# Two layers of a hybrid decoder on one core: index products in pairs of banks, and a head with its loads, gates and decay rows at other places

## The chip, the cores and the metric

The kernel runs on one core of one Trainium2 chip. A core has five engines, each with its own queue of instructions: TensorE (PE, matrix products and transposes), VectorE (DVE, element-wise work and reductions), ScalarE (ACT, functions and copies), GpSimd (POOL) and SyncE (SP), which issues the DMA transfers. An engine runs its queue in order; where an instruction needs another engine's result, it waits on a semaphore, and everything behind it in its queue waits too. TensorE's results land in PSUM banks, from which ACT and DVE read them. The metric is the device time of one launch in microseconds (us), lower is better.

## The reference, cut to what matters

Two layers, each a token mixer and a SwiGLU feed-forward part, over 256 tokens of width 1024. Each is normed and scaled by a conditioning vector, which is the product of `silu(c)` with `w_mod`:

```python
mod = c_act @ w_mod[l] + b_mod[l]               # 1024 x 6144 per layer
sh_m, sc_m, g_m, sh_f, sc_f, g_f = jnp.split(mod, 6, axis=-1)
h = rms_norm(x, mix_norm_pre[l]) * (1.0 + sc_m[:, None, :]) + sh_m[:, None, :]
y = hybrid_mixer(h, ...)
```

The mixer joins eight attention heads with four mLSTM heads. The attention looks only at 64 keys per query, which an indexer picks; the index has eight heads of depth 64:

```python
idx_logits = jnp.einsum('thd,sd->ths', qib, ki32)
idx_score = jnp.einsum('ths,th->ts', jax.nn.relu(idx_logits), wib)
idx_score = jnp.where(key_pos[None, :] <= t[:, None], idx_score, -jnp.inf)
_, sel = lax.top_k(idx_score, n_sel)            # n_sel = 64, blocks of 128 queries
```

The mLSTM heads need, per token, an input gate and the running sum of a log forget gate, from which a running maximum (the "stabiliser") and a matrix of decays follow.

## The kernel before, in words

**Head of a layer (L449 to L603).** `mixer` first issues what the gates, index and queries need. `between(n)` (called at several places) fetches the next pieces of `w_mod` (1 MB each, tile `wm`, two rows of 1024 per partition) and multiplies them into an accumulator `macc` with one DVE operation per row: L189 for the first row of a block, L191 (a multiply and add) for the others. `HEAD[l]` says how many pieces each such call takes. In order there come: the product `pki` (index keys and gate columns, weights `wsm`), its copy `kix`, the rotary product `kir`, the transposes `pwif`, then the gate block (transposes `pgt`, gates `ga`/`gc`, two scans, the maximum `M`, its rounded copy `Mp` and the remainder), the keys' product `pka` in two halves (`k_att(0,0)`, `k_att(0,1)`, weights `wka`), and the query products `pqidx` and `pq` (weights `wup`) with their rotary parts. A rotary part is a copy on ACT (`...x`), a product with `perm` on PE (`...p`), a product with `cosT` on POOL or DVE, one with `sinT` on DVE (`...b`, L358) and an addition (L359). The second transfer of keys' weights, the pieces of the next conditioning block, and the weights `wqk` come behind these.

**Order.** The rest of the layer is written as a list of steps (`ORDER[l]`): `w` is `decays()`, `e` is `k_att(1, m)`, `v` is a product of values, `i` the top-k of one block of queries, `r` the keys' rotary part, `l`, `t`, `u` the attention's logits, weights and products. A mark `~` says whether a step may start before the last matmul of the step ahead of it in the order of issue. The order on each engine is settled when the program is built: a scheduler with a model of durations places every instruction.

**Index products (L637 to L660).** For 128 queries of block `i` and 128·(i+1) keys, `index_part(i, b)` fills one PSUM bank `pi` of 512 columns: four heads of block 0, or two of block 1; a head's 64 rows lie in the lower or the upper half of the partitions (`p0 = 64 * (hd % 2)`). ACT takes the bank through a Relu (`rl`, L651), and DVE adds each head, times its weight, to the score `sc` (L656, L658). `inside` (L843) calls six of these, each after two of the 16 steps of a product of keys (layer 0) or values (layer 1). The order of heads is `HEADS[i]`. The top-k is a chain of pairs MAX8 and MATCH_REPLACE8 on DVE (L668, L669), eight per block of queries; the attention's logits `pl` are masked into `lm` (L709), their maximum `mx` taken (L712), and the exponentials go to the transposes `pT`.

**Decay rows (L609 to L634).** `decays()` transposes the gates (`pu`), copies them (`uc`), and multiplies the rows `Mp` with a selection (`pM`); ACT makes the decays `W` from `pM`.

Of the kernel before, what the change touches and what calls it, by code (L numbers as in the profile page):

```python
# [11 lines left out]
F32 = mybir.dt.float32  # L12
# [7 lines left out]
P = 128  # L20
# [36 lines left out]
def tile_hybrid_decoder(ctx: ExitStack, tc: tile.TileContext, a, out):  # L57
# [384 lines left out]
    HEAD = ((2, 2, 1, 1), (3, 2, 1, 0, 0))  # L442
# [3 lines left out]
    def mixer(l, h, between, early, hook, hf=None):  # L446
# [112 lines left out]
        k_att(0, 0)  # L559
        k_att(0, 1)  # L560
# [48 lines left out]
        def decays():  # L609
            pu = bankA(nm + "pu")  # L610
# [26 lines left out]
        def index_part(i, b):  # L637
            w_ = P * (i + 1)
            per = 512 // w_
            h0 = b * per  # L640
            if b == 0:
                score[i] = work.tile([P, S], F32, tag="score", name=f"{nm}sc{i}")
            sc = score[i]
            ps = bankA(f"{nm}pi{i}{h0}")
            for g in range(per):
                hd = HEADS[i][h0 + g]
                p0 = 64 * (hd % 2)
                mm = matmul(ps[:, g * w_:(g + 1) * w_], qT["qidx"][p0:p0 + 64, hd // 2, i * P:(i + 1) * P],
                                      kidx[p0:p0 + 64, 0, :w_], start=True, stop=True)
            rl = t2k(f"{nm}rl{i}{h0}")  # L650
            nc.scalar.activation(rl, ps, AF.Relu)  # L651
            for g in range(per):
                hd = HEADS[i][h0 + g]
                s = rl[:, g * w_:(g + 1) * w_]
                if h0 + g == 0:
                    nc.vector.tensor_scalar_mul(sc[:, :w_], s, wi[:, i, hd:hd + 1])  # L656
                else:
                    nc.vector.scalar_tensor_tensor(sc[:, :w_], s, wi[:, i, hd:hd + 1], sc[:, :w_], op0=ALU.mult, op1=ALU.add)  # L658
            return mm
# [183 lines left out]
        inside = {2 * b + 2: (lambda b=b: index_part(*((0, b) if b < 2 else (1, b - 2)))) for b in range(6)}  # L843
# [247 lines left out]
```

## Time and profile before

| what | value |
|---|---|
| median of 3 runs | 736.84 us (734.61 to 737.44) |
| the profiled execution | 737.16 us, of which the trace spans 735.4 us |
| PE busy | 705.0 us (96%) |
| DVE busy | 546.5 us (74%) |
| ACT busy | 347.8 us (47%) |
| POOL busy | 105.0 us (14%) |
| chain that ended last | PE 75%, DVE 10%, DMA 6%, issue 3% |
| mean granted TensorE clock | 0.992 of full speed |

PE is busy nearly all the span, so a wait of PE is the first thing to look for; there are few, and they are listed in the first group below. But a busy share is an average: stretches in which DVE has no idle time lie inside it. A timeline row gives a start, a duration, an engine, a line and operation, output and inputs, and in brackets the idle time before it with what ended it; where several instructions of one form follow one another they share a row (`x8`). PE's rows overlap by the length of the pipeline, so the distance from start to start tells more than a duration.

### The profile page before, as it was taken

The numbers are of one execution on the slowest core, as the hardware profiler recorded it, in microseconds if no ns is written. First come the engines' busy times: TensorE is split into PE (matmuls) and PEld (weight loads), VectorE is DVE, ScalarE is ACT, GpSimd is POOL, SyncE is SP. The second block draws the span as 40 slices with busy tenths as digits, with TensorE's granted clock in tenths as the row PEclk, the third lists the DMA queues.
The fourth block names the chain that finished last, engine by engine and source line by source line (L and its number), as shares of the span: only waits on it lengthen the run. The fifth ranks groups of instructions, "written<-read, shape, count | busy, mean of one in ns | idle before, by whom it ended". The sixth has DMA issues, their size and how long they took to land.

```text
span 735.4 us, 11666 instructions
## 1 busy us (share of the span) xinstructions
PE 705.0 (96%) x4597; PEld 623.2 (85%) x4597; DVE 546.5 (74%) x856; ACT 347.8 (47%) x613; POOL 105.0 (14%) x93
## 2 busy tenths in 40 slices
PE   3997999999999999999999989999999999999996
PEld 3555777888799999999988877999889999999995
DVE  3667788985998647797988899987777675655553
ACT  6021224665664444444536534686774444444442
POOL 1000520101000022210011253632210000000010
PEclk9998999999999999999999999999999999999999
DMA  9999973494969956989793933344536487664001
GB/s 305 349 293 355 365 255 105 164 323 155 313 218 314 322 208 230 338 293 342 245 375 96 329 119 115 119 151 134 178 136 226 161 303 258 216 212 172 1 1 57
DMA packets 106202, 162.77 MB, mean 221 GB/s; under 512 B 7634, under 2 KB 83998, under 8 KB 106148
## 3 DMA queue, kind: packets, MB, share of 16 engines
q1 hardware_dynamic: 106148, 162.04, 64.7%
q8 instruction: 36, 0.59, 0.3%
q14 instruction: 18, 0.15, 0.1%
HBM read 160.98 MB, written 1.05 MB: 220 GB/s over the span
## 4 chain that ended last, share of the span: by engine, by line
PE 75%; DVE 10%; DMA 6%; issue 3%; ACT 2%; SPq 1%; POOL 1%; DVEq 0%; POOLq 0%; ACTq 0%
PE f0pu L111 8%; PE f1pu L111 8%; PE f0pg L111 8%; PE f1pg L111 8%; PE f1y L111 7%; PE f0y L111 7%; PE m1pqk L111 3%; PE m1y L111 3%; DMA m0wcq<-in_w_in_dram 3%; PE m0pka L111 2%; PE m0y L111 2%; PE m1pva L111 2%; PE m1pom L111 1%; DMA wq<-in_w_mod_dram 1%; PE m1pka L111 1%
## 5 line engine op out<-in xcount | busy, mean ns | idle before, releaser
L191 DVE SCALAR_TENSOR_TENSOR macc<-wm,ccol,macc 128x1024 f32<-128x1024 f32 x70 | 94.3, 1347 | 11.3 <-DMA wm<-in_w_mod_dram 10.6
L254 POOL TENSOR_TENSOR macc<-macc,br 1x512 f32<-1x512 f32 x6 | 10.0, 1670 | 166.4 <-DMA br<-in_b_mod_dram 142.9
L111 PE MATMUL m0pqk<-n0hf,m0wqk 128*128 128x256 f32 x128 | 29.4, 382 | 0.0
L111 PEld LDWEIGHTS m0pqk<-n0hf,m0wqk 128*128 128x128 f32 x128 | 23.8, 191 | 3.6 <-issue 0.5
L205 DVE SCALAR_TENSOR_TENSOR macc<-wq,ccol,macc 128x512 f32<-128x512 f32 x28 | 21.1, 752 | 3.3 <-DMA wq<-in_w_mod_dram 2.1
L111 PE MATMUL m0pka<-n0hf,m0wka 128*128 128x256 f32 x64 | 18.1, 430 | 3.6 <-DMA m0wka<-in_w_in_dram 3.6
L111 PEld LDWEIGHTS m0pka<-n0hf,m0wka 128*128 128x128 f32 x64 | 13.0, 214 | 7.5 <-DVE macc L191 3.7
L990 ACT ACTIVATE n0hf<-n0xT,mod,A 128x256 f32<-128x256 f32 x7 | 3.9, 594 | 30.5 <-DVE A L216 30.5
L111 PE MATMUL pvm<-m0wvm,n0hf 128*128 128x512 f32 x32 | 15.9, 645 | 1.1 <-ACT n0hf L990 1.1
L111 PE MATMUL m0pom<-m0wom,n0hf 128*128 128x256 f32 x64 | 14.5, 380 | 0.0
L111 PE MATMUL pva<-m0wva,n0hf 128*128 128x512 f32 x32 | 14.4, 593 | 0.0
L111 PEld LDWEIGHTS pvm<-m0wvm,n0hf 128*128 128x128 f32 x32 | 6.6, 211 | 7.9 <-issue 6.0
L715 ACT ACTIVATE m0lm<-m0lm,m0mx 128x128 f32<-128x128 f32 (+1 forms) x16 | 7.1, 446 | 13.2 <-DVE m0mx L712 13.2
L189 DVE TENSOR_SCALAR macc<-wm,ccol 128x1024 f32<-128x1024 f32 x10 | 8.9, 889 | 5.9 <-DMA wm<-in_w_mod_dram 4.7
L876 DVE TENSOR_TENSOR f1t<-f1pu,f1s 128x512 f32<-128x512 f32 x11 | 7.6, 691 | 7.5 <-PE f1pu L111 6.0
L111 PEld LDWEIGHTS m0pom<-m0wom,n0hf 128*128 128x128 f32 x64 | 11.9, 191 | 1.4
L258 POOL TENSOR_TENSOR ml<-macc,mh 128x512 fp32r<-128x512 f32 x6 | 9.3, 1546 | 24.4 <-ACT mh L256 24.4
L111 PEld LDWEIGHTS pva<-m0wva,n0hf 128*128 128x128 f32 x32 | 6.1, 190 | 7.6 <-issue 7.6
L886 ACT CAST f0th<-f0t 128x512 fp32r<-128x512 f32 x10 | 6.2, 620 | 11.8 <-DVE f0t L876 11.8
L774 DVE SCALAR_TENSOR_TENSOR m1cv<-m1pqk,vc,m1cv 128x255 f32<-128x255 f32 (+2 forms) x24 | 11.1, 476 | 0.5 <-ACT m1cv L768 0.3
L356 POOL TENSOR_TENSOR m0qidx<-m0rqidx0x,cosT 128x512 f32<-128x512 f32 x1 | 1.3, 1266 | 70.0 <-ACT m0rqidx0x L90 70.0
L774 DVE SCALAR_TENSOR_TENSOR m0cv<-m0pqk,vc,m0cv 128x255 f32<-128x255 f32 (+2 forms) x24 | 11.0, 476 | 0.2
(1824 smaller groups left out, 2781.2 us busy)
## 6 DMA issues: line engine op xcount, KB each, us to landing
wm<-in_w_mod_dram SPq DMA_DIRECT2D x40, 1024.0 KB
f0wd<-in_w_down_dram SPq DMA_DIRECT2D x11, 1024.0 KB
f1wd<-in_w_down_dram SPq DMA_DIRECT2D x11, 1024.0 KB
f0wg<-in_w_gate_up_dram SPq DMA_DIRECT2D x10, 1024.0 KB
f0wu<-in_w_gate_up_dram SPq DMA_DIRECT2D x10, 1024.0 KB
f1wg<-in_w_gate_up_dram SPq DMA_DIRECT2D x10, 1024.0 KB
f1wu<-in_w_gate_up_dram SPq DMA_DIRECT2D x10, 1024.0 KB
wq<-in_w_mod_dram SPq DMA_DIRECT2D x32, 256.0 KB
```

The source lines that it names most:

```text
L111: final["pe"] = nc.tensor.matmul(*args, **kw)
L189: nc.vector.tensor_scalar_mul(acc, w[:, kk, :], ccol[:, k:k + 1])
L191: nc.vector.scalar_tensor_tensor(acc, w[:, kk, :], ccol[:, k:k + 1], acc, op0=ALU.mult, op1=ALU.add)
L205: last = nc.vector.scalar_tensor_tensor(acc, w[:, kk, :], ccol[:, k:k + 1], acc, op0=ALU.mult, op1=ALU.add)
L254: nc.gpsimd.tensor_tensor(acc[0:1, :], acc[0:1, :], br[0:1, :], op=ALU.add)
L258: nc.gpsimd.tensor_tensor(lo, acc, hi.bitcast(F32), op=ALU.subtract)
L356: (nc.vector if nm + "c" in OTHER else nc.gpsimd).tensor_tensor(dst, r3(xs, 2), cb, op=ALU.mult)
L715: final["exp"] = nc.scalar.activation(lm[:, g, :], lm[:, g, :], AF.Exp, bias=mx[:, g:g + 1], accum_out=den[:, hd:hd + 1])
L774: nc.vector.scalar_tensor_tensor(o[:, d:], s[:, :S - d], V["conv_w"][:, tap * 8 + j:tap * 8 + j + 1], o[:, d:], op0=ALU.mult, op1=ALU.add)
L876: nc.vector.tensor_mul(t, pu, s)
L886: nc.scalar.copy(th[:, 0], r3(t, 2))
L990: nc.scalar.activation(hf[:, j, :], s, AF.Identity, scale=A, bias=b)
```

## The change

Four edits, in `mixer`. The conditioning pieces at the head of layer 0 are taken in the numbers 0, 2, 2, 2 instead of 2, 2, 1, 1, and the keys' first weights are issued ahead of the second of these calls (in layer 0 alone). The gate block moves behind the first half of the keys' product, in both layers. The rows `Mp` (an ACT copy and a DVE subtraction) move into `decays()`. The index products go to two banks in turn, in three visits after steps 2, 6 and 10 instead of six after every second step.

```diff
-    HEAD = ((2, 2, 1, 1), (3, 2, 1, 0, 0))
+    HEAD = ((0, 2, 2, 2), (3, 2, 1, 0, 0))
...
+        raw0 = None if l else load_cols(win, C_KA, f"{nm}wka0")
         between(HEAD[l][1], bool(l))
-        raw0 = load_cols(win, C_KA, f"{nm}wka0")
+        raw0 = load_cols(win, C_KA, f"{nm}wka0") if l else raw0
...
+        k_att(0, 0)
         pg = bankA(nm + "pgt")
         for i in range(NT):
             for g in range(2):
...
         nc.vector.tensor_add(lf, t0, M)
-        nc.scalar.copy(Mp[0:MH, :], M)
-        nc.vector.tensor_tensor(Mp[32:32 + MH, :], M, Mp[0:MH, :].bitcast(F32), op=ALU.subtract)
...
-        k_att(0, 0)
         k_att(0, 1)
         between(HEAD[l][2], bool(l))
...
         def decays():
+            nc.scalar.copy(Mp[0:MH, :], M)
+            nc.vector.tensor_tensor(Mp[32:32 + MH, :], M, Mp[0:MH, :].bitcast(F32), op=ALU.subtract)
             pu = bankA(nm + "pu")
...
-        def index_part(i, b):
+        def index_pair(i, q):
             w_ = P * (i + 1)
             per = 512 // w_
-            h0 = b * per
-            if b == 0:
+            if q == 0:
                 score[i] = work.tile([P, S], F32, tag="score", name=f"{nm}sc{i}")
             sc = score[i]
-            ps = bankA(f"{nm}pi{i}{h0}")
+            banks = [(2 * q + j) * per for j in range(2)]
+            pss = [bankA(f"{nm}pi{i}{h0}") for h0 in banks]
             for g in range(per):
-                hd = HEADS[i][h0 + g]
-                p0 = 64 * (hd % 2)
-                mm = matmul(ps[:, g * w_:(g + 1) * w_], qT["qidx"][p0:p0 + 64, hd // 2, i * P:(i + 1) * P],
-                                      kidx[p0:p0 + 64, 0, :w_], start=True, stop=True)
-            rl = t2k(f"{nm}rl{i}{h0}")
-            nc.scalar.activation(rl, ps, AF.Relu)
...
+                for ps, h0 in zip(pss, banks):
+                    hd = HEADS[i][h0 + g]
+                    p0 = 64 * (hd % 2)
+                    mm = matmul(ps[:, g * w_:(g + 1) * w_], qT["qidx"][p0:p0 + 64, hd // 2, i * P:(i + 1) * P],
+                                kidx[p0:p0 + 64, 0, :w_], start=True, stop=True)
+            for ps, h0 in zip(pss, banks):
+                rl = t2k(f"{nm}rl{i}{h0}")
+                nc.scalar.activation(rl, ps, AF.Relu)
...
-        inside = {2 * b + 2: (lambda b=b: index_part(*((0, b) if b < 2 else (1, b - 2)))) for b in range(6)}
+        inside = {2: lambda: index_pair(0, 0), 6: lambda: index_pair(1, 0), 10: lambda: index_pair(1, 1)}
```

On SP's queue, which issues the transfers, this is the head of layer 0 before (`wm` a conditioning piece, `wka` the keys' weights, `wup` the queries'):

```order
39 L82 DMA wm_386<-in_w_mod_dram 128x2x1024
40 L82 DMA wm_390<-in_w_mod_dram 128x2x1024
41 L468 DMA m0wsm<-in_w_in_dram 128x8x72
42 L469 DMA m0wsm<-in_w_in_dram 128x8x8
43 L82 DMA wm_428<-in_w_mod_dram 128x2x1024
44 L82 DMA wm_432<-in_w_mod_dram 128x2x1024
45 L82 DMA m0wka_436<-in_w_in_dram 128x8x256
46 L557 DMA m0wup<-in_w_qidx_up_dram 128x2x512
```

And the same place of SP's queue in the changed kernel:

```order
39 L468 DMA m0wsm<-in_w_in_dram 128x8x72
40 L469 DMA m0wsm<-in_w_in_dram 128x8x8
41 L82 DMA m0wka_419<-in_w_in_dram 128x8x256
42 L82 DMA wm_422<-in_w_mod_dram 128x2x1024
43 L82 DMA wm_426<-in_w_mod_dram 128x2x1024
44 L538 DMA m0wup<-in_w_qidx_up_dram 128x2x512
45 L539 DMA m0wup<-in_w_q_up_dram 128x2x512
46 L82 DMA wm_487<-in_w_mod_dram 128x2x1024
```

Four pieces stood ahead of the keys' weights and none does now; the same pieces follow behind the weights.

On PE, the index products of layer 0 before (`pi` the banks, `pka` the keys' second product, in whose steps they lie):

```order
53 L111 MATMUL m0pi_620<-m0kidx,m0qidx 128x128 x4
54 L111 MATMUL m0pka_614<-n0hf,m0wka_615 128x256 x2
55 L111 MATMUL m0pi_633<-m0kidx,m0qidx 128x128 x4
56 L111 MATMUL m0pka_614<-n0hf,m0wka_615 128x256 x2
57 L111 MATMUL m0pi_647<-m0kidx,m0qidx 128x256 x2
58 L111 MATMUL m0pka_614<-n0hf,m0wka_615 128x256 x2
```

And the same place on PE in the changed kernel:

```order
52 L111 MATMUL m0pi_620<-m0kidx,m0qidx 128x128 x3
53 L111 MATMUL m0pi_621<-m0kidx,m0qidx 128x128 x3
54 L111 MATMUL m0pi_620<-m0kidx,m0qidx 128x128
55 L111 MATMUL m0pi_621<-m0kidx,m0qidx 128x128
56 L111 MATMUL m0pka_614<-n0hf,m0wka_615 128x256 x4
57 L111 MATMUL m0pi_647<-m0kidx,m0qidx 128x256
58 L111 MATMUL m0pi_648<-m0kidx,m0qidx 128x256
59 L111 MATMUL m0pi_647<-m0kidx,m0qidx 128x256
60 L111 MATMUL m0pi_648<-m0kidx,m0qidx 128x256
61 L111 MATMUL m0pka_614<-n0hf,m0wka_615 128x256 x4
```

Block 1's two banks alternate from one matmul to the next; the pair of block 0 stands as three, three, one and one.

On DVE, the end of the rotary parts of layer 0 before (L191 with `macc` is conditioning, `sc` the score):

```order
64 L358 TENSOR_TENSOR m0rqidx1b<-m0rqidx1p,sinT 128x512
65 L359 TENSOR_TENSOR m0qidx<-m0qidx,m0rqidx1b 128x512
66 L191 SCALAR_TENSOR_TENSOR macc_497<-wm_717,ccol,macc_497 128x1024
67 L358 TENSOR_TENSOR m0rq0b<-m0rq0p,sinT 128x512
68 L191 SCALAR_TENSOR_TENSOR macc_497<-wm_717,ccol,macc_497 128x1024
69 L358 TENSOR_TENSOR m0rq1b<-m0rq1p,sinT 128x512
70 L615 COPY m0uc<-m0pu 128x8
71 L359 TENSOR_TENSOR m0q<-m0q,m0rq1b 128x512
72 L358 TENSOR_TENSOR m0rka0b<-m0rka0p,sinT 128x512
73 L359 TENSOR_TENSOR m0kT<-m0kT,m0rka0b 128x512
74 L656 TENSOR_SCALAR m0sc_619<-m0rl_625,m0wi 128x128
```

And the same place on DVE in the changed kernel:

```order
63 L359 TENSOR_TENSOR m0qidx<-m0qidx,m0rqidx1b 128x512
64 L189 TENSOR_SCALAR macc_563<-wm_564,ccol 128x1024
65 L358 TENSOR_TENSOR m0rq0b<-m0rq0p,sinT 128x512
66 L191 SCALAR_TENSOR_TENSOR macc_563<-wm_564,ccol,macc_563 128x1024
67 L358 TENSOR_TENSOR m0rq1b<-m0rq1p,sinT 128x512
68 L191 SCALAR_TENSOR_TENSOR macc_563<-wm_568,ccol,macc_563 128x1024
69 L359 TENSOR_TENSOR m0q<-m0q,m0rq1b 128x512
70 L191 SCALAR_TENSOR_TENSOR macc_563<-wm_568,ccol,macc_563 128x1024
71 L616 COPY m0uc<-m0pu 128x8
72 L358 TENSOR_TENSOR m0rka0b<-m0rka0p,sinT 128x512
73 L359 TENSOR_TENSOR m0kT<-m0kT,m0rka0b 128x512
74 L191 SCALAR_TENSOR_TENSOR macc_563<-wm_717,ccol,macc_563 128x1024 x2
```

Two conditioning operations stood in this stretch and six do now; the first score operation follows them.

## Rows read from the trace of the kernel before

**Rows 1.** PE's waits in the whole span: line waited for, us, times, longest.

```profile
PE m0pka L111 <- DMA m0wka<-in_w_in_dram: 3.6, 1, 3.6
PE m1rq0p L111 <- ACT m1rq0x L90: 2.2, 1, 2.2
...
PE m1pgt L115 <- DVE m1wif L512: 1.0, 1, 1.0
PE m0pT L115 <- ACT m0lm L715: 0.8, 1, 0.8
```

**Rows 2.** Stretches: busy us of PE, PEld, DVE, ACT, POOL; granted clock, DMA, GB/s.

```profile
64.50:71.50 7.00, 5.18 (x14) 3.93 (x15) 4.47 (x11) 0.83 (x2) 0.00 (x0) 0.51 1.04 397
56.77:93.17 36.40, 31.92 (x134) 23.48 (x134) 27.96 (x40) 8.80 (x22) 11.44 (x9) 0.91 1.05 373
93.17:117.71 24.54, 24.34 (x113) 18.29 (x112) 22.27 (x70) 3.57 (x6) 3.17 (x7) 1.00 0.50 175
432.00:438.00 6.00, 5.23 (x20) 3.62 (x21) 5.72 (x11) 2.47 (x5) 3.44 (x3) 0.72 0.60 178
438.00:475.00 37.00, 37.00 (x272) 32.30 (x271) 35.69 (x88) 18.83 (x43) 16.59 (x15) 1.00 0.32 114
```

**Rows 3.** Timeline of PE at the head of layer 0.

```profile
57.21 3.65 PE L111 MATMUL m0pki<-n0hf,m0wsm 128*80 128x256 f32 x16 [0.48 <-DMA m0wsm<-in_w_in_dram]
61.32 1.13 PE L111 MATMUL m0kir<-m0kix,dup 64*128 64x256 f32 x4 [0.46 <-ACT m0kix L90]
...
66.32 1.19 PE L111 MATMUL m0pka<-n0hf,m0wka 128*128 128x256 f32 x2 [3.58 <-DMA m0wka<-in_w_in_dram]
...
68.16 8.27 PE L111 MATMUL m0pka<-n0hf,m0wka 128*128 128x256 f32 x30
```

**Rows 4.** Timeline of PE in layer 0, index products to attention weights.

```profile
91.06 1.16 PE L111 MATMUL m0pi<-m0kidx,m0qidx 64*128 64x128 f32 x8
...
95.35 1.13 PE L111 MATMUL m0pi<-m0kidx,m0qidx 64*128 64x256 f32 x4
...
106.45 5.78 PE L111 MATMUL m0pqk<-n0hf,m0wqk 128*128 128x256 f32 x26
...
118.29 1.48 PE L115 MATMUL m0pT<-ident,m0lm 128*128 128x128 f32 x4 [0.78 <-ACT m0lm L715]
119.70 1.14 PE L111 MATMUL m0pl<-m0kT,m0q 64*128 64x256 f32 x8
```

**Rows 5.** Timeline of DVE in layer 0: conditioning, score, top-k and logits.

```profile
54.03 1.29 DVE L191 SCALAR_TENSOR_TENSOR macc<-wm,ccol,macc 128x1024 f32<-128x1024 f32 x1
56.77 0.23 DVE L174 COPY vc<-pvec 128x74 f32<-128x74 f32 x1 [1.46 <-PE pvec L115]
...
87.60 1.69 DVE L191 SCALAR_TENSOR_TENSOR macc<-wm,ccol,macc 128x1024 f32<-128x1024 f32 x1
...
93.17 0.29 DVE L656 TENSOR_SCALAR m0sc<-m0rl,m0wi 128x128 f32<-128x128 f32 x1 [0.17 <-ACT m0rl L651]
...
95.40 1.13 DVE L658 SCALAR_TENSOR_TENSOR m0sc<-m0rl,m0wi,m0sc 128x128 f32<-128x128 f32 x3 [0.73 <-ACT m0rl L651]
...
103.50 0.48 DVE L658 SCALAR_TENSOR_TENSOR m0sc<-m0rl,m0wi,m0sc 128x256 f32<-128x256 f32 x1 [0.78 <-ACT m0rl L651]
...
110.64 0.43 DVE L668 MAX8 m0m<-m0sc 128x8 f32<-128x256 f32 x1
...
111.63 0.43 DVE L668 MAX8 m0m<-m0sc 128x8 f32<-128x256 f32 x1
...
116.50 1.21 DVE L712 TENSOR_REDUCE m0mx<-m0lm 128x8 f32<-128x1024 f32 x1
...
120.94 0.75 DVE L709 SCALAR_TENSOR_TENSOR m0lm<-m0pl,m0rs,m0mk 128x512 f32<-128x512 f32 x1 [2.05 <-PE m0pl L111]
```

**Rows 6.** Timeline of POOL at the rotary parts of layer 0.

```profile
86.64 1.56 POOL L356 TENSOR_TENSOR m0q<-m0rq1x,cosT 128x512 f32<-128x512 f32 x1 [1.31 <-ACT m0rq1x L90]
```

**Rows 7.** Timeline of DVE in layer 1: a conditioning row.

```profile
441.98 3.41 DVE L191 SCALAR_TENSOR_TENSOR macc<-wm,ccol,macc 128x1024 f32<-128x1024 f32 x1
```

More of the change, by code (lines that the diff above doesn't have):

```diff
@@ L559, in mixer @@
         k_att(0, 0)
+        pg = bankA(nm + "pgt")
+        for i in range(NT):
+            for g in range(2):
+                transpose(pg[:MH, g * S + i * P:g * S + (i + 1) * P], wif[:, i, 8 + 4 * g:12 + 4 * g], ident)
+        M = keep.tile([MH, S], F32, tag="M", name=nm + "M")
+        ga, gc = (t2k(nm + n) for n in ("ga", "gc"))
+        u, lf, t0 = ga[:MH, 0:S], ga[:MH, S:], gc[:MH, 0:S]
+        gb = V["gate_b"]
+        nc.vector.tensor_scalar(u, pg[:MH, 0:S], gb[:, 0:1], None, op0=ALU.add)
+        nc.vector.tensor_scalar(lf, pg[:MH, S:2 * S], gb[:, 1:2], None, op0=ALU.add)
+        nc.vector.scalar_tensor_tensor(t0, lf, -1.0, lf, op0=ALU.mult, op1=ALU.max)
+        nc.scalar.activation(t0, t0, AF.Exp, scale=-1.0)
+        nc.scalar.activation(t0, t0, AF.Ln, bias=1.0)
+        nc.vector.scalar_tensor_tensor(lf, lf, 0.0, t0, op0=ALU.min, op1=ALU.subtract)
+        nc.vector.tensor_tensor_scan(t0, one4, lf, 0.0, op0=ALU.mult, op1=ALU.add)
+        nc.vector.tensor_sub(u, u, t0)
+        nc.vector.tensor_tensor_scan(M, one4, u, 0.0, op0=ALU.mult, op1=ALU.max)
+        nc.vector.tensor_add(lf, t0, M)
         k_att(0, 1)
@@ L635, in mixer @@
         mask, score = [], {}
-        def index_part(i, b):
+        def index_pair(i, q):
             w_ = P * (i + 1)
             per = 512 // w_
-            h0 = b * per
-            if b == 0:
+            if q == 0:
                 score[i] = work.tile([P, S], F32, tag="score", name=f"{nm}sc{i}")
             sc = score[i]
-            ps = bankA(f"{nm}pi{i}{h0}")
+            banks = [(2 * q + j) * per for j in range(2)]
+            pss = [bankA(f"{nm}pi{i}{h0}") for h0 in banks]
             for g in range(per):
-                hd = HEADS[i][h0 + g]
-                p0 = 64 * (hd % 2)
-                mm = matmul(ps[:, g * w_:(g + 1) * w_], qT["qidx"][p0:p0 + 64, hd // 2, i * P:(i + 1) * P],
-                                      kidx[p0:p0 + 64, 0, :w_], start=True, stop=True)
-            rl = t2k(f"{nm}rl{i}{h0}")
-            nc.scalar.activation(rl, ps, AF.Relu)
[L652 to L658, printed above, removed]
+                for ps, h0 in zip(pss, banks):
[6 more added lines that the diff above has]
+                nc.scalar.activation(rl, ps, AF.Relu)
+                for g in range(per):
+                    hd = HEADS[i][h0 + g]
+                    s = rl[:, g * w_:(g + 1) * w_]
+                    if h0 + g == 0:
+                        nc.vector.tensor_scalar_mul(sc[:, :w_], s, wi[:, i, hd:hd + 1])
+                    else:
+                        nc.vector.scalar_tensor_tensor(sc[:, :w_], s, wi[:, i, hd:hd + 1], sc[:, :w_], op0=ALU.mult, op1=ALU.add)
             return mm
```

18 lines of the change are left out of this document (removed).

## The prediction, made before the changed kernel ran

> **What bounds the kernel now.** I read PE's waits first. PE is busy for 96% of the span, so a gain must take away a wait of PE or shorten its work. The reader is to see that four waits lie where the edits are: 3.6 us for the keys' weights and 0.8 us for the attention's exponentials in layer 0, 1.0 us for the gate columns and 2.2 us for a rotary copy in layer 1 [rows 1]. The last one isn't touched. Then I read busy time by stretch, because a share of 96% hides who is last in a stage. From 56.77 to 93.17 DVE works 27.96 of 36.40 us and stands idle for 8.44; from 93.17, the first score operation, to 117.71, the end of the logits' maximum, it works 22.27 of 24.54; in layer 1 from 438 to 475 it works 35.69 of 37.00 [rows 2]. So two engines are nearly full at once. Last I read the two timelines, PE's and DVE's, from the head of layer 0 to the attention weights `pT`: PE waits there for ACT's exponential, and that for the maximum on DVE, which ends at 116.50 + 1.21 = 117.71 [rows 4, 5]. PE has its products done 0.78 us earlier. In layer 0, therefore, the end is set by DVE, and what PE saves ahead of 117.71 is worth only what it lets DVE start earlier.
>
> **Loads and gates at the head of layer 0.** The keys' weights pass four conditioning pieces on SP's queue, 4 MB. At 373 GB/s [rows 2] four pieces take 4 × 1.05 / 0.373 = 11 us, so the weights land long before PE asks for them, 3.58 us ahead of 66.32 [rows 3]; the small weights `wsm` pass two pieces, and their wait of 0.48 us goes too [rows 3]. The half-speed stretch that comes with the long wait should go with it: the granted clock is 0.51 from 64.5 to 71.5, that is the level of 1.2 GHz [rows 2]. There 30 records of `pka` took 8.27 us [rows 3], while 26 records of the same shape took 5.78 us at full clock, 0.222 each [rows 4]; 30 would take 6.67, so 1.6 us were lost. PE saves 3.58 + 0.48 + 1.6 = 5.7 us. The pieces come later, but the stream is full in either order and carries the same bytes, so the second keys' weights, behind the same pieces, land when they did; I cost the loads at nothing. Should a piece come late, DVE would wait, and PE behind it, by at most one piece, 2.8 us.
>
> DVE gets none of that for nothing. The first two rows of a conditioning block run now before 56.77, in time that DVE has free; afterwards they come behind it. That adds 0.75 (the first row, taken as 0.6 of the second's) and 1.29 us [rows 5], 2.0 in all, to the 27.96 us. The waits that stay on DVE I put at 5.1 us: for the key-index product 3.0 (PE starts `pki` at 56.7 without its wait, `kir` 4.1 us later and ends it at 61.9 [rows 3], and DVE is through with its first piece at 59), for the transposed gates 0.4, ACT's two functions 0.9, the reciprocal root 0.6, a POOL result 0.2. The small gaps between instructions, 0.8 us, stay. Sum: 56.77 + 27.96 + 2.0 + 5.1 + 0.8 = 92.6. The first score operation starts 0.5 us earlier than 93.17. The bounds are wide, since the order is new: 1.6 us earlier if half of the small waits are covered, 3 us later if the conditioning rows are stretched by POOL.
>
> For that last bound there is a row. In the rotary stretch a conditioning row took 1.69 us beside a POOL product of 1.56 us, against 1.29 alone [rows 5, 6], and in layer 1 one took 3.41 us, 2.1 more [rows 7]. The change puts six such rows where two stood, beside POOL's products. The Trainium skill (GPSIMD Engine Reference, Specifications) says that POOL's paths to SBUF are shared with VectorE, with contention where a VectorE instruction reads two tensors from SBUF; a conditioning row does (piece and accumulator). The trace agrees with it as far as these two rows go. By the rule each of the four added rows that meets POOL is stretched, up to what rival (c) makes of it; without the rule none is. I take 0.4 for one or two of them within the sum, as it stands in the 27.96 already.
>
> **Index products in pairs.** A bank takes 1.13 to 1.16 us now, six of them some 6.8 us. That lower and upper halves in two banks run together is shown where the logits do it already: `pl`, 8 records with two heads in either half, took 1.14 us, as long as 4 records of `pi` with all heads in one half [rows 4]. Block 1's two pairs then save 2 × 1.13 = 2.3 us; block 0's pair, in layer 0 not strictly in turn, between 0 and 1.2, taken as 0.6. PE saves 2.9 us in layer 0 and 2 × 1.13 + 1.16 = 3.4 in layer 1, where all pairs alternate. Behind PE the work is unchanged: six Relus and 16 score operations at the same lengths. On DVE two waits for a Relu, 0.73 and 0.78 us [rows 5], lie between the visits; with two banks at a time and PE ahead, both go: 1.5 us. Bounds 0 and 1.5.
>
> The Trainium skill (TensorEngine Tiling (Array Packing), PSUM Bottleneck) says that tiling speeds up the products but not the emptying of PSUM. By this rule alone the pairs are worth nothing; by the rows they are worth the 1.5 us of DVE's idle time out of PE's 2.9. No run here has yet the pair itself.
>
> **Top-k.** DVE runs the seventh top-k pair of block 1 ahead of the maximum now; in the changed order it comes behind it. A pair takes 111.63 − 110.64 = 0.99 us [rows 5]. The maximum gains 1.0 us, and the pair falls into the 2.05 us that DVE waits for the next logits [rows 5], so it costs nothing there.
>
> **Layer 0.** The maximum comes 0.5 + 1.5 + 1.0 = 3.0 us earlier, and `pT` with it. PE is there 5.7 + 2.9 us earlier less what it waits for DVE on the way, so its wait grows from 0.78 to some 3 us. Then it may fall to half clock: after the wait of 3.58 us it did [rows 1, 2], and the stretch with the wait of 2.22 shows 0.72 [rows 1, 2]. The next products, `pT` and `pl`, took 1.48 and 1.14 us; at half clock they take up to 1.3 us more. DVE's wait behind them has 1.0 us of top-k inside now. I take 0.3, between 0 and 1.6 (what 30 records lost above). Layer 0: −2.7 us. What lies behind runs both engines full, so the shift stays.
>
> **Layer 1.** The gate transposes wait 1.00 us for the gate columns [rows 1]; with half of the keys' product ahead of them that wait is filled, and the chain of gates behind it, down to the copy that ends the 2.2 us wait, moves up by 1.0 us. The decay rows' move changes little, because ACT's cast stays ahead of that copy. The 3.4 us of the pairs meet a DVE that has 1.3 us free out of 37 [rows 2], so PE waits for DVE instead, at the decay products or at `pT`. I take 0 for them, between −1.3 and +1.5 (a new fall of the clock). Layer 1: −1.0.
>
> **Sum.** −2.7 − 1.0 = −3.7 us. The profiled execution, 737.16 us, would come to 733.5; it stands 0.3 above the median, from which the same gives 736.84 − 3.7 = 733.1.
>
> **Rivals.** (a) *More of PE's time counts.* If DVE's limit is looser than the sum says, all of PE's savings arrive: 5.7 + 2.9 + 1.0 + 3.4 = 13.0 us, 723.8; half of it gives 730.3. For it: the whole span is PE's at 96%. Against it: the idle time of DVE in these stretches [rows 2]. I put it at half, 730.3. (b) *DVE takes it all back, or the pairs don't run in turn as meant.* The first score operation starts when it did, the wait at `pT` costs 1.6 us of half clock, and layer 1's wait only moves to the next place: −1.5 − 1.0 + 1.6 = −0.9 us, 735.9. For it: 35.69 of 37.00 us in layer 1, and block 0's pair in 3, 3, 1, 1. Against it: the top-k pair is moved for certain. (c) *Slower: conditioning against POOL.* The rows moved into the rotary stretch are stretched as that of layer 1: four at 2.1 us add 8.5 us, less the 3.7 gained is +4.8, 741.6. The place is DVE between 75 and 93 us; it decides from the point where the rows cost 3.7 us in all, two of them. For it: the two stretched rows [rows 5, 7]. It is what the rule of the Trainium skill on POOL's paths, above, would do here at its worst. Against it: in the rotary stretch POOL's products are half as wide as the one that may stand behind the 3.41 us, and the one row that met one lost only 0.4.
>
> **How the numbers follow.** What a measurement of this kernel can tell from no change is about 0.5%, 3.7 us: faster means below 733.2, slower above 740.5. My forecast, 0.46, own range 731 to 735.5, lies on the border: half of it is faster. Case (a) 0.25, faster; (b) 0.19, the same; (c) 0.10, nearly all slower. Faster 0.23 + 0.25 = 0.48; same 0.23 + 0.19 + 0.01 = 0.43; slower 0.09. The range goes from 727, beyond the half of (a), to 738.5, beyond (b) and into the way to (c); the whole of (a) and of (c) stays out.
>
> **What would show it.** Right: no wait for `m0wka` and a granted clock of 1.0 from 64 to 72; `pi` pairs of block 1 in 1.1 us; the first score operation near 92.6 and the maximum's end near 114.7; PE's wait at `m0pT` at 2 to 4 us; no wait at `m1pgt`, and new waits of PE for DVE in layer 1. Wrong: conditioning rows above 1.7 us beside POOL, a wait of DVE for a piece `wm`, a score that starts after 93.2, or a PE that reaches `m0pT` later than DVE.

## The result: slower, 741.1 us, and the profile after

The changed kernel takes 741.13 us (median of 5, 740.29 to 741.93); the kernel before, with two more runs, 735.35 (734.46 to 737.44). The ratio is 1.0073 [1.0052, 1.0094]: it is slower by 0.7%, outside the range of the prediction and on the other side. The profiled execution took 740.29 us (span 738.6), 3.1 us over the profiled execution of before.

The waits of PE in the changed kernel (columns as in [rows 1]):

```profile
PE m0pT L115 <- ACT m0lm L718: 4.2, 1, 4.2
...
PE m1pM L111 <- DVE m1rka0b L358: 3.3, 1, 3.3
PE m0pM L111 <- DVE m0rq0b L358: 3.2, 1, 3.2
PE m1rq0p L111 <- ACT m1rq0x L90: 2.4, 1, 2.4
...
PE m1rqidx0p L111 <- ACT m1rqidx0x L90: 1.3, 1, 1.3
```

All waits of [rows 1] that were to go are gone: for `m0wka` and for the gate columns. The one at `m0pT` has grown from 0.8 to 4.2 us, and five new ones of 1.0 us or more have come. The two longest are at the decay products `pM` of either layer, for DVE; the others, of 1.0 to 1.3 us, are for ACT (`m1rqidx0p`, and the first index product of layer 0) and for DVE (`m0rka0p`).

Stretches of the changed kernel (columns as in [rows 2]); the first and the third lie between the same events as those of [rows 2] that start at 56.77 and 93.17:

```profile
56.58:94.84 38.26, 32.52 (x148) 23.67 (x148) 33.31 (x43) 9.29 (x23) 14.27 (x10) 0.91 0.98 349
83.00:90.00 7.00, 4.38 (x8) 2.35 (x8) 7.00 (x8) 0.00 (x0) 4.37 (x2) 0.51 0.93 301
94.84:117.69 22.85, 19.24 (x100) 15.14 (x96) 22.01 (x68) 2.75 (x5) 3.96 (x6) 0.99 0.43 144
117.00:124.00 7.00, 5.73 (x21) 4.12 (x22) 4.34 (x12) 5.16 (x20) 0.29 (x1) 0.51 0.47 148
458.00:466.00 8.00, 5.33 (x26) 5.11 (x27) 8.00 (x23) 1.71 (x7) 4.95 (x5) 0.57 0.00 0
```

DVE is busy for 33.31 us ahead of the first score operation, against 27.96 in [rows 2]. And the granted clock is at the level of 1.2 GHz (0.51, or 0.57 where the stretch is cut a little wide) in three stretches, at 83, 117 and 458 us. They begin within PE's three longest waits: at `m0pM` (81 to 84 us), at `m0pT` (114 to 118 us; ACT waits there for DVE's maximum) and at `m1pM` (457 to 461 us). Behind the 2.4 us at `m1rq0p` the clock stayed at full speed in this profile. In [rows 2] it was low at 64 (0.51) and, for part of the stretch, from 432 to 438 (0.72).

DVE in layer 0 of the changed kernel, then POOL (timelines):

```profile
73.17 1.38 DVE L610 TENSOR_TENSOR Mp<-m0M,Mp 4x256 fp32r<-4x256 f32 x1
74.58 2.18 DVE L191 SCALAR_TENSOR_TENSOR macc<-wm,ccol,macc 128x1024 f32<-128x1024 f32 x1
...
80.04 1.22 DVE L589 TENSOR_SCALAR m0rs<-m0rqr 128x2 f32<-128x2 f32 x1 [0.22 <-POOL m0rqr L276]
81.17 1.44 DVE L592 TENSOR_SCALAR m0wi<-m0wif,m0rqr 128x8 f32<-128x8 f32 x2
...
87.79 1.75 DVE L359 TENSOR_TENSOR m0q<-m0q,m0rq1b 128x512 f32<-128x512 f32 x1
...
94.84 0.42 DVE L659 TENSOR_SCALAR m0sc<-m0rl,m0wi 128x128 f32<-128x128 f32 x1
...
116.48 1.21 DVE L715 TENSOR_REDUCE m0mx<-m0lm 128x8 f32<-128x1024 f32 x1
...
122.35 0.75 DVE L712 SCALAR_TENSOR_TENSOR m0lm<-m0pl,m0rs,m0mk 128x512 f32<-128x512 f32 x1 [2.49 <-PE m0pl L111]
```

```profile
71.69 2.58 POOL L356 TENSOR_TENSOR m0qidx<-m0rqidx0x,cosT 128x512 f32<-128x512 f32 x1 [62.92 <-ACT m0rqidx0x L90]
...
79.97 1.26 POOL L356 TENSOR_TENSOR m0q<-m0rq0x,cosT 128x512 f32<-128x512 f32 x1
81.19 1.26 POOL L356 TENSOR_TENSOR m0q<-m0rq1x,cosT 128x512 f32<-128x512 f32 x1
...
86.75 2.24 POOL L356 TENSOR_TENSOR m0kT<-m0rka0x,cosT 128x512 f32<-128x512 f32 x1
```

Five operations on DVE are long: a subtraction of 4x256, which takes 0.41 elsewhere, takes 1.38; a conditioning row 2.18; two small ones on 2 and 8 columns 1.22 and 1.44; a sum of 512 columns 1.75. All of them lie beside POOL's products, and the operations held up end about when POOL's product does: `rs` at 81.26, the product that starts at 79.97 at 81.23. The first score operation starts at 94.84 (93.17 in [rows 5]), and the maximum `mx` at 116.48, where it was (116.50).

PE in layer 0 of the changed kernel:

```profile
61.71 3.66 PE L111 MATMUL m0pka<-n0hf,m0wka 128*128 128x256 f32 x16
...
94.47 1.13 PE L111 MATMUL m0pi<-m0kidx,m0qidx 64*128 64x256 f32 x8
...
118.27 0.47 PE L115 MATMUL m0pT<-ident,m0lm 128*128 128x128 f32 x1 [4.19 <-ACT m0lm L718]
...
120.17 2.09 PE L111 MATMUL m0pl<-m0kT,m0q 64*128 64x256 f32 x8
```

The keys' product starts without a wait. A pair of banks of block 1 takes 1.13 us, as long as one bank in [rows 4]. The transposes `pT` wait 4.19 us, and the logits behind them take 2.09 us instead of 1.14 [rows 4], at half clock.

### The profile page after: what moved, and what is told of

It reads as the page before. It is cut to its first block, busy times and chain, and to the rows that moved or that the text cites. A ratio compares the mean times of both kernels' runs of the same rounds, so it can differ in the third digit from the quotient of the medians.

```text
span 738.6 us, 11660 instructions
## 1 busy us (share of the span) xinstructions
PE 699.9 (95%) x4597; PEld 620.3 (84%) x4597; DVE 551.9 (75%) x856; ACT 347.3 (47%) x613; POOL 108.5 (15%) x93
## 4 chain that ended last, share of the span: by engine, by line
PE 74%; DVE 16%; issue 4%; ACT 3%; POOL 2%; DMA 1%; DVEq 0%; POOLq 0%; SPq 0%; ACTq 0%
PE f0pu L111 8%; PE f1pu L111 8%; PE f0pg L111 8%; PE f1pg L111 8%; PE f1y L111 7%; PE f0y L111 7%; PE m1pqk L111 3%; PE m1y L111 3%; DVE macc L191 3%; PE pvm L111 2%; PE m0y L111 2%; PE pva L111 2%; PE m1pom L111 1%; PE m0pom L111 1%; PE m0pcq L111 1%
## 5 line engine op out<-in xcount | busy, mean ns | idle before, releaser
L191 DVE SCALAR_TENSOR_TENSOR macc<-wm,ccol,macc 128x1024 f32<-128x1024 f32 x70 | 94.1, 1344 | 9.7 <-DMA wm<-in_w_mod_dram 9.1
L111 PEld LDWEIGHTS m0pqk<-n0hf,m0wqk 128*128 128x128 f32 x128 | 24.5, 196 | 3.6 <-issue 0.5
L111 PE MATMUL m0pka<-n0hf,m0wka 128*128 128x256 f32 x64 | 15.9, 399 | 0.0
```

The costliest lines, as they stand in the source:

```text
L111: final["pe"] = nc.tensor.matmul(*args, **kw)
L191: nc.vector.scalar_tensor_tensor(acc, w[:, kk, :], ccol[:, k:k + 1], acc, op0=ALU.mult, op1=ALU.add)
```

## The experiments

The theories, as the expectations name them: **A**, DVE and POOL hold each other up, and the head edit puts DVE's rows beside POOL's products; **B**, the half clock behind longer waits of PE; **C** or **G**, the gates. The table gives, from the timelines, how much later than in the first profile of before a stage starts: the score and the maximum on DVE, layer 0's output product; "layer 1" is what is added between its first product (`m1pki`) and the feed-forward part behind it. The last column has the medians, with the median of before measured beside it.

| kernel | score | maximum | `m0y` | layer 1 | median (before) |
|---|---|---|---|---|---|
| changed | +1.7 | 0.0 | +2.1 | +1.4 | 741.1 (735.4) |
| head edit alone | +1.0 | +0.1 | +1.5 | −0.5 | 738.7 (736.1) |
| pairs alone | −1.0 | −2.7 | −1.2 | −1.1 | 734.8 (736.1) |
| pairs alone, again | −2.3 | −3.7 | −2.3 | +0.9 | 735.4 (736.0) |
| gates and decay rows alone | +3.9 | +15.1 | +15.1 | +0.4 | 751.0 (736.1) |
| changed, head edit undone | +1.3 | −0.4 | +1.1 | +1.6 | 740.6 (736.1) |
| changed, gates undone | +1.8 | +2.3 | +3.7 | −1.3 | 737.3 (736.1) |
| changed, gates in layer 0 only | +3.8 | +3.2 | +4.5 | +0.1 | 739.5 (736.3) |
| changed, rotary part on DVE | +1.0 | +1.3 | +2.2 | −0.1 | 739.4 (736.1) |
| before, profiled again | −1.0 | −1.0 | −1.0 | +0.2 | one run, 735.9 |
| changed, profiled again | +1.3 | −0.3 | +1.8 | +1.5 | one run, 740.5 |

Each row is one profiled execution. The two of before differ by 1.0 us in the first three columns, the two of the pairs alone by 1.0 to 1.3 there and by 1.9 in layer 1, so a difference of a microsecond in one column tells nothing by itself. DVE's busy time up to the first score operation repeats better: 27.96 us in both profiles of before, 33.31 and 33.33 in those of the changed kernel. In two rows (gates in layer 0 only, rotary part on DVE) PE waits at 45 us for a sum of conditioning (1.9 and 1.4 us), ahead of all edits, and layer 0's first product starts about 2 us later; that much of their first three columns has nothing to do with the edits.

**Each edit by itself.**

```diff
 # e1: before, with
-    HEAD = ((2, 2, 1, 1), ...
+    HEAD = ((0, 2, 2, 2), ...      # and raw0 ahead of the second between()
 # e2: before, with index_pair and inside = {2: ..., 6: ..., 10: ...}
 # e3: before, with k_att(0, 0) ahead of the gate block and Mp in decays()
 # e4: changed, with HEAD[0] = (2, 2, 1, 1) and raw0 behind between()
```

> The kernel before with the head edit alone (conditioning pieces 0, 2, 2, 2 and the keys' first weights ahead of them). Theory A (DVE and POOL hold each other up where both read two tensors from SBUF, and the head edit fills DVE's idle time beside POOL's rotary products): the first score operation starts later than 93.2, at 94 to 95.5, although PE's 3.6 us wait is gone; time 1 to 3 us over before. Theory B (the half clock after the long wait at the attention weights is the whole loss): the score starts at 92 to 93, the time moves by less than 1 us, because without the pairs PE's wait there stays near 2 us. Theory C (layer 1's gates are the loss): the time is 1 to 3 us under before.

The head edit alone, 738.67, ratio 1.0039 [1.0018, 1.0060]: A is met in both numbers. DVE's busy time in this kernel, between the same events as above:

```profile
56.33:94.14 37.81, 32.56 (x143) 23.61 (x142) 33.26 (x43) 8.89 (x23) 13.39 (x10) 0.91 1.03 371
```

33.26 us: the same as in the changed kernel. The head edit alone is enough for all of it.

> The kernel before with the index pairs alone. A: DVE gains its two waits of 0.73 and 0.78 us in layer 0, the maximum ends 1 to 2.5 us earlier than 117.7, time 1 to 2 us under before. B: PE arrives some 3.5 us earlier at the attention weights, waits 2 to 4 us, the clock falls to half behind it and the time is 1 to 2 us over before. C: no change in layer 0 worth a measurement, within 1 us.

> The kernel before with the pairs alone, once more, beside the two runs above: 733.5 to 735.5, 0.5 to 2 us under before, if the first result holds.

The pairs alone, 734.84, ratio 0.9982 [0.9967, 0.9996]; once more they gave 735.44, 0.9991 [0.9978, 1.0003]. The maximum comes 2.7 us earlier, as A has it. Between the maximum and `m0y` 1.5 us are lost again, with a half-speed stretch behind the 2.5 us wait at `pT`; the run below that fills this wait puts some 0.9 us of them down to it. The time that B forecast, 1 to 2 us over before, did not come. As a version it beats the changed kernel; over before the gain is 0.1 to 0.2%, and the second interval includes none at all.

> The kernel before with the gate block behind the first half of the keys' product and the decay rows in decays(), in both layers. A: layer 1 loses 1 to 1.5 us, since the gate transposes come 0.8 us later and the key-index addition on DVE then falls beside POOL's subtraction (2.5 us instead of 0.4); layer 0 within 0.5 us; time about 1 us over before. B: within 0.5 us of before. C (the gates of layer 1 cost more than the 1 us seen): 2 us or more over before.

The gates alone, 751.0, ratio 1.0194 [1.0175, 1.0212]: none of the three saw this. DVE waits 6.44 us for the gates, as the transposes now stand behind half a product that starts after its own 3.6 us wait, at half clock. PE then waits twice for DVE ahead of the index products, and what follows is the largest loss of the study. The gates on DVE, PE's index products and their stretch in this kernel:

```profile
73.27 0.47 DVE L548 TENSOR_SCALAR m0ga<-m0pgt,gb 4x256 f32<-4x256 f32 x1 [6.44 <-PE m0pgt L115]
```

```profile
92.46 1.91 PE L111 MATMUL m0rka0p<-m0rka0x,perm 128*128 128x512 f32 x2 [0.76 <-DVE m0uc L615]
94.30 2.08 PE L111 MATMUL m0pi<-m0kidx,m0qidx 64*128 64x128 f32 x8
...
114.34 2.07 PE L111 MATMUL m0pi<-m0kidx,m0qidx 64*128 64x256 f32 x4
```

```profile
92.00:117.00 25.00, 24.54 (x56) 15.03 (x57) 11.69 (x28) 6.21 (x15) 4.71 (x7) 0.51 0.39 142
```

Every visit to a bank takes 2.07 us instead of 1.13 [rows 4], with 0.51 of the clock for 25 us on end. PE is busy in it for 24.54 us: it is hardly waiting any more, and still the clock doesn't rise before the last visit is over (at 116 us; it does at 119).

> The changed kernel with the head edit undone (pairs, gates and decay rows stay). A: DVE has its idle time back beside POOL's products; the first score operation starts near 93, the attention weights' maximum ends 1 to 2.5 us earlier than 117.7, and the time is 2 to 4 us under the changed kernel, 737 to 739. B: the wait at the attention weights is 1 to 3 us as PE no longer gains its 5.7 us, the clock stays, 738 to 740. C: the time stays at the changed kernel's, 740 to 742.

The head edit undone, 740.64: no better than the changed kernel, so the expectation of A fails. The time is in the range of C; B's is missed, and the clock did not stay as B has it (half clock from 119 to 123 us). In layer 0 the gates take the head edit's place: DVE is busy for 29.38 us only, but waits 5.02 us for the transposed gates, and the score is as late. So either edit is enough to make layer 0 late, the head edit by DVE's rows beside POOL's, the gates by a wait of DVE. Layer 1 loses 1.6 us, against 1.4 in the changed kernel.

**Who pays in layer 1, and in layer 0's rotary stretch.**

```diff
 # h: changed, the gate block ahead of k_att(0, 0) and Mp behind the gates, as before
 # g1: changed, the gate block ahead of k_att(0, 0) in layer 1 alone
 # x1: changed, with the rotary products of layer 0 on DVE
-OTHER = frozenset("... m0rq0a ...")
+OTHER = frozenset("m0rqidx0c m0rqidx1c m0rq0c m0rq1c m0rka0c m0rka1c ...")
```

> The changed kernel with the gate block and the decay rows back at their places of before, in both layers (head edit and pairs stay). Theory G (the gate block behind half of the keys' product is the loss, above all together with the pairs): layer 1 ends as in the run with the pairs alone, 2.6 us earlier relative to layer 0's end than in the run with the head undone, and the time is 735 to 737.5. Theory A (the head edit, DVE beside POOL): layer 0 still loses, the first score operation at 94 or later, time 737.5 to 740. Both can hold in part; 741 or more refutes G.

737.26, ratio 1.0030 [1.0011, 1.0048]: 3.9 us under the changed kernel. G holds in layer 1 (−1.3 instead of +1.4), though not all of these 2.7 us are the gates': the clock fell at another place too (see below). Between profiles in which it fell at the same place, the gates make 1.1 us (against the run with the rotary part on DVE) to 1.4 (the next run, against changed). A holds in layer 0, where the loss is still there, and larger; the half clock of 84 to 98 us runs into the index products there.

> The changed kernel with the gate block at its old place in layer 1 alone. Theory G: layer 1's maximum scan starts 1.0 us earlier against its layer's start, as in the runs without the moved gates; with it go 1.0 us, and another 1.5 where the half-speed stretch at 458 to 466 goes too: 738 to 740. Rival (the order of the rest of the layer, not the gates' place): within 0.5 us of the changed kernel.

739.52, within G's range, though the half-speed stretch didn't go: it is at 462 to 467. The scan of the maximum starts 0.9 us earlier against its layer, and layer 1 ends 1.4 us earlier.

> The changed kernel with all of layer 0's rotary products and the one rotary sum of POOL done by DVE (six products of 0.68 us and a sum more on DVE, 4.8 us of work; POOL idle there). Theory A (DVE and POOL take turns at two-tensor reads, so a POOL product beside a full DVE costs DVE its whole 1.3 us): the first score operation comes at the same time or earlier, 92.5 to 95, no small DVE operation takes over 0.8 us, and the time is 738 to 741. Rival (POOL's products cost DVE nothing, the rows are long for another reason): DVE gets 4.8 us more work, the score starts at 98 to 100 and the time is 743 to 746.

739.35, ratio 1.0047 [1.0030, 1.0064] against the changed kernel's 1.0073 [1.0052, 1.0094]: hardly apart in time, but clear in DVE's rows. With five more products and a sum of 0.68 us each on DVE ahead of the score, DVE is busy not longer but 3 us less:

```profile
58.47:94.16 35.69, 30.92 (x136) 22.79 (x134) 30.36 (x48) 8.91 (x22) 4.04 (x5) 0.91 1.03 368
435.00:440.00 5.00, 3.88 (x11) 2.40 (x12) 4.78 (x9) 2.05 (x4) 3.79 (x3) 0.66 0.67 213
457.00:466.00 9.00, 7.48 (x54) 6.06 (x53) 9.00 (x28) 3.18 (x9) 4.63 (x5) 1.00 0.00 0
```

The first row against 33.31: POOL is busy for 4.04 instead of 14.27 us, and no small operation of DVE takes over 0.8 us. The one that took 1.22 us above:

```profile
80.50 0.17 DVE L589 TENSOR_SCALAR m0rs<-m0rqr 128x2 f32<-128x2 f32 x1 [0.60 <-POOL m0rqr L276]
```

So POOL's products beside DVE's rows cost DVE some 5.5 us: 3.0 us of busy time less, although about 3.8 us were added; 1.3 us of the difference is a conditioning row that moved behind the first score operation. That is A's mechanism by itself. The time did not gain as much, as PE waits 4.3 us at `m0pM` in this profile and runs at half clock from 87 to 97 us.

**The clock.** In the pairs alone and their repetition the program is the same, and layer 1 differs by 1.9 us. The stretches and one wait of the first and of the second:

```profile
56.72:92.16 35.44, 30.91 (x141) 23.02 (x142) 28.19 (x41) 8.85 (x23) 12.15 (x9) 0.95 1.05 373
431.00:436.00 5.00, 4.64 (x16) 3.03 (x17) 4.72 (x9) 2.06 (x4) 3.03 (x3) 0.66 0.66 211
453.00:463.00 10.00, 8.64 (x66) 7.28 (x67) 9.96 (x30) 4.37 (x12) 6.46 (x8) 1.00 0.09 6
...
PE m1pM L111 <- DVE m1rka0b L358: 1.4, 1, 1.4
```

```profile
430.00:435.00 5.00, 4.76 (x30) 3.76 (x31) 4.72 (x9) 1.85 (x4) 2.94 (x3) 1.00 0.64 209
453.00:461.00 8.00, 5.58 (x26) 5.36 (x27) 7.93 (x23) 1.96 (x8) 5.21 (x6) 0.57 0.00 0
...
PE m1pM L111 <- DVE m1rka0b L358: 3.3, 1, 3.3
```

In the first the clock is low (0.66) at 431 to 436, behind the wait of 2.2 us at `m1rq0p`; PE comes later to `m1pM`, waits 1.4 us there, and the clock stays at 1.00. In the second the wait at `m1rq0p` is the same, but the clock is at 1.00 behind it; PE comes earlier, waits 3.3 us, and then runs at half clock (0.57 from 453 to 461). The changed kernel has the second pattern in both its profiles, the one with the rotary part on DVE the first (its second and third row above), and their layers 1 differ by 1.6 us. Leave out the inconclusive run with filled waits below, and of the twelve profiles of kernels with pairs, five have the first pattern (a fall between 431 and 440, then 1.2 to 1.5 us at `m1pM`) and seven the second (3.2 to 3.3 us at `m1pM`, half clock from 453 to 466 behind it). So the two go together in every one of them; that the early fall spares the later one is how I read it, and no run tests it.

```diff
 # f1: e2, f2: changed; ahead of the transposes of the first weights of layer 0
+            for _ in range(4):                       # f2: 8
+                matmul(pt[:, 0:S], ident, cosT, start=True, stop=True)
 # f1 and f2 also: k01~ ahead of t00 in ORDER[0], t00 without its mark; f2 six of these ahead of layer 1's first pM
```

> The kernel before with the pairs, and four products of no use (128x256, some 1.7 us) on PE ahead of the attention weights of layer 0, in the wait of 2.5 us. Theory B (the half clock behind the wait takes the gain of the pairs back in layer 0): the granted clock stays 1.0 from 114 to 125, and the time falls by 1 to 1.8 us under the run with the pairs alone, 733 to 734. Rival: the clock isn't what ends that stretch; the time stays within 0.5 us of it, or rises.

736.04: a miss as a whole, and within the noise of before (ratio 0.9998). No half clock at `pT`, and from the maximum to `m0y` 0.9 us less than in the pairs alone, so B holds there. Two things stand against the gain in its profile: the score started 1.5 us later than in the pairs alone, and the wait at `m1pM` was 3.3 us, with the half clock behind it. The repetition of the pairs had that second pattern without any added product, so the run doesn't decide what filling a wait brings.

> The changed kernel with eight such products (3.4 us) in the wait of 4.2 us at layer 0's attention weights and six (2.6 us) ahead of the decay products of layer 1, where PE waits 3.3 us. Theory B: no half-speed stretch at 117 to 124 and at 458 to 466; 2 us come back in layer 0 and 1 to 1.5 in layer 1, time 737 to 738.5. Rival (DVE sets both ends, the clock only fills idle time): 740.5 to 742.

747.74, inconclusive: the added products made the scheduler place other work anew (the convolutions on DVE go ahead of the logits, PE waits 2.3 us for one of them in layer 1).

**Can the conditioning go elsewhere?**

```diff
 # c1, c2: e2 with HEAD[0] = (2, 2, 1, 0) and (2, 2, 0, 0), one and two b1~ behind o01/n1 in ORDER[0]; c2 also a further d
 # r4: before, r1: e2, with raw0 ahead of the second between() and HEAD as before
```

> The kernel before with the pairs, and one conditioning piece of layer 0's head taken behind the mLSTM's products instead (numbers 2, 2, 1, 0 at the head, one more piece behind step n1). Theory A (in layer 0 DVE's work ahead of the attention weights sets the end): two conditioning rows fewer, 2.6 us, so the maximum ends 2 to 2.6 us earlier than with the pairs alone (115.0), PE's wait of 2.5 us at the weights goes to 0 to 1 us, the clock stays there, and the time falls to 731 to 733.5. Rival (the stretch behind the weights is as full for DVE, so the moved rows cost there what they gain here): within 0.7 us of the pairs alone.

> The same with two pieces taken later (numbers 2, 2, 0, 0). Theory A: PE becomes the one that arrives last at the weights, so the second piece brings at most 1 us more than the first, 730.5 to 733. Rival: as for the first piece; or the rows now collide with the mLSTM's work behind it and the time rises above that of one piece.

742.68 and 735.37 (before 736.27). With two pieces later the maximum comes 3.8 us earlier and `m0y` 5.0, and 2.4 us of it are lost again at the end of the layer, where the late block is waited for. With one, a block closes at a worse place: PE waits 1.9 us for its column sums and 2.2 for ACT in the mLSTM part, and `m0y` is 8.4 us late. Neither beats the pairs alone.

> The kernel before with the keys' first weights issued ahead of the second pair of conditioning pieces, all numbers of pieces as before (2, 2, 1, 1). Theory A (not the transfers' order but the rows pushed beside POOL's products cost): DVE keeps its first two pieces ahead of 56.8 us, PE's wait of 3.6 us and its half clock go, the gates start some 3 us earlier, and the first score operation comes at 91 to 93; time 0 to 2.5 us under before. Rival (PE's lead itself does the harm: longer waits behind, more half clock): 1 to 3 us over before, as the whole head edit.

> The same with the pairs. Theory A: 1 to 2 us under the pairs alone (732.5 to 734). Rival: PE's longer waits bring the half clock, 735 to 738.

749.65 and 740.15: the rival is right in direction, but its ranges are missed too; the first is 13.7 us over before, where it had 1 to 3. Without the wait for `m0wka` PE waits 3.2 us at `m0pM` for DVE, and the half clock begins there. Two rows of the first kernel:

```profile
87.01 0.76 PE L111 MATMUL m0pM<-Mp,sel 36*128 36x256 f32 x2 [3.18 <-DVE m0rqidx1b L358]
...
94.11 2.07 PE L111 MATMUL m0pka<-n0hf,m0wka 128*128 128x256 f32 x4
```

Single banks at half clock again, up to 117 us (PE busy for 25.00 of the 25.00 us from 92 on, clock 0.51); with the pairs the half clock ends at 100. The order of the transfers is as before but for one load, and still the score is 1.7 us late: DVE is busy for 31.48 us ahead of it instead of 27.96, and I read that as its rows beside POOL's, since PE, and POOL with it, runs ahead. The maximum is 12.4 us late; the difference lies in the stretch at half clock.

**The profiles again.**

> The kernel before, unchanged, profiled once more, to see which half-speed stretches of PE come in every execution. If they hang on the kernel alone: 64 to 72 and 433 to 437 again, every stage within 0.2 us of the first profile. If they hang on how the waits fall: the stretches have other lengths or places, and the stages behind them move by 0.5 to 2 us.

> The changed kernel, unchanged, profiled once more. If its half-speed stretches hang on the waits of the kernel: again behind the waits at the attention weights (117 to 124) and at layer 1's decay products (458 to 466), with starts moved by a few us at most; 740 to 742.

735.88 and 740.49. In the second profile of before the stretches at half clock start 1 us earlier and the head is 1.0 us shorter; the changed kernel repeats its stages to 0.4 us, with the same three stretches:

```profile
82.00:90.00 8.00, 4.46 (x8) 2.35 (x8) 8.00 (x10) 0.00 (x0) 4.49 (x3) 0.57 1.06 361
116.00:124.00 8.00, 6.05 (x22) 4.42 (x23) 5.33 (x13) 5.18 (x20) 0.29 (x1) 0.57 0.43 133
458.00:465.00 7.00, 4.61 (x20) 4.39 (x21) 7.00 (x22) 0.99 (x4) 4.47 (x4) 0.51 0.00 0
```

So the first profile of before was a long one of its kind, and the distance of the second profiles, 4.6 us, is nearer to that of the medians than the 3.1 of the first.

## Why the prediction was wrong, point by point

**PE's gain at the head (5.7 us) and the pairs (1.1 us each).** Right, and the head rather too small: `m0rq0p` starts 7.2 us earlier, since more of the work ahead of it than I counted had run at half clock. A pair takes 1.13 us.

**DVE's sum to the first score.** The step that failed first. The two moved rows (2.0 us) came out, and the waits and gaps, 5.9 in the sum, are 4.95 us of idle time. The term for DVE's rows beside POOL, "I take 0.4 for one or two of them within the sum, as it stands in the 27.96 already", did not: it put nothing on top, and the busy time is 33.31, which is 27.96 + 2.0 and 3.4 more. The five operations above hold it. Together they take 5.1 us longer than the same five with POOL's rotary products moved to DVE; before, rows of this stretch had lost about 1.1 us already. The chosen value lay at the wrong end of the bound ("3 us later if the conditioning rows are stretched by POOL"): the score starts at 94.84 instead of 92.6. I had looked for the price in the conditioning rows alone; but small operations with one tensor on DVE were held up for a microsecond as well (`rs`, 0.17 to 1.22), so every row beside POOL may count. With DVE nearly full, some 5.5 of POOL's 14.3 us came on top of DVE's own. The Trainium skill (GPSIMD Engine Reference, Specifications) names both cases, instructions with two inputs from SBUF and those in a mode with two ports; I cited the half of it that the shown rows bore out. That the small operations run in that mode is not shown here; the run with the rotary part on DVE shows the size.

**Relu waits and top-k (2.5 us).** From the score to the maximum's end it was 22.85 us instead of 24.54: 1.7 gained and not 2.5, since a conditioning row beside POOL (2.08 us at 105.3) took 0.8 back. Together with the score, 2.2 us later than forecast, the maximum stayed where it was, and the 3.0 us of layer 0 were gone.

**The clock at `pT` (0.3 us).** Mis-sized. The wait came out as 4.19 us, of the forecast kind and a little over the forecast 2 to 4; its half clock lasted from 117 to 124. From the maximum to `m0y` it took 2.1 us longer than before, where I had 0.3. Not all of that is the clock: the run with the rotary part on DVE, without half clock there, still lost 0.8, so some 1.3 us are the clock's, and the rest is open. I had charged it to the two products behind the wait and let DVE's wait cover it.

**Layer 1 (−1.0).** Wrong in sign, in the step "with half of the keys' product ahead of them that wait is filled, and the chain of gates behind it moves up by 1.0 us". Half the product is 24 matmuls in layer 1. Seven of them stood ahead of the transposes before, beside the wait of 1.0 us; the other 17 take 1.9 us, more than the wait they fill. The transposes came 0.8 us later against the layer, not earlier, and so the next sum on DVE met POOL. Before, changed on DVE, changed on POOL:

```profile
418.59 0.40 DVE L507 TENSOR_TENSOR m1kidx<-m1kidx,m1kib 128x256 f32<-128x256 f32 x1
...
429.55 2.25 DVE L530 TENSOR_TENSOR_SCAN m1M<-ones,m1ga 4x256 f32<-4x256 f32 x1
```

```profile
419.97 2.50 DVE L508 TENSOR_TENSOR m1kidx<-m1kidx,m1kib 128x256 f32<-128x256 f32 x1
...
432.26 2.25 DVE L557 TENSOR_TENSOR_SCAN m1M<-ones,m1ga 4x256 f32<-4x256 f32 x1
```

```profile
419.79 2.40 POOL L101 TENSOR_TENSOR m1wka11l<-m1wka,m1wka11h 128x1024 fp32r<-128x1024 f32 x1 [11.71 <-ACT m1wka11h L90]
```

0.40 us became 2.50, and the scan for the maximum, the last DVE row of either, starts 1.1 us later against the layer. That is about what the gates cost by the runs with and without them in layer 1, 1.1 to 1.4 us. The pairs gave layer 1 1.1 us where the clock fell early, at 431. Where it fell at `m1pM` instead, layer 1 was longer by 1.6 us (changed, against the rotary part on DVE) or 1.9 (the pairs, twice).

By the profiles, then, the change lost against its forecast 2.2 us at the score, 0.8 in the stretch to the maximum, 1.8 from there to `m0y`, and 2.4 in layer 1.

**Rivals.** The time was that of (c), 741.6, and so was part of its cause: the place, DVE between 75 and 93 us, and DVE's rows beside POOL's. But its price was 3.4 us, not 8.5, and most of it fell on small operations and a sum, not on the conditioning rows it names; the rest of the loss was layer 0 behind the maximum and layer 1. That the times agree is luck. I gave it 0.10.

What stays open: what exactly keeps the clock low through single banks and lets it rise in pairs, and whether the changed kernel without its half-speed stretches would beat before. No run takes the stretches away and leaves the order alone, so the clock's part of the loss is argued from differences between runs, not shown by one.

## What to carry to other kernels

Before conditioning or other rows are moved into a stretch, add up the busy time of DVE and POOL there. Where DVE had idle time, before, POOL's 11.4 us cost it some 1.1; in the changed kernel, where DVE was nearly full, 5.5 of POOL's 14.3 us were paid on DVE. A saved wait of PE is worth nothing if PE then waits for the same late engine further on, and it may cost more than it saved when the clock falls at that later wait; so look for the wait that follows. Filling a wait with a block longer than the wait delays what stood behind it.

## What was not expected of the hardware

After a wait of PE, index products of 64 rows into a single bank in turn with full products ran at 0.51 of the clock for 25 us though PE was busy for 24.5 and 25.0 of them (the gates alone and the earlier weights alone, both with single banks and a late DVE). Where such a stretch ran into pairs of banks, it was over by 98 to 100 us of the span (the pairs with the earlier weights, and the changed kernel with the gates undone, with the gates in layer 0 only or with the rotary part on DVE). And layer 1 was shorter where the clock fell early in it, by 1.9 us between two profiles of one program and by 1.0 to 1.6 between others; that the early fall spares a longer wait later is a reading, not tested. A subtraction, two small operations and a sum on DVE, beside POOL's products, each took about 1 us longer than without them; `rs` on two columns ended when POOL's product did.
